# Token tiles of even and of odd tokens as the stationary operand of four projections in a hybrid encoder block

## The chip, the cores and the metric

One NeuronCore of a Trainium2 chip runs the whole block as one program. The metric is the device time of one execution in microseconds (us); the times shown are the median of several executions and their spread. A trace of one profiled execution lists every instruction of the engines: PE (TensorE, the matmuls), PEld (TensorE's weight loads, which overlap PE), DVE (VectorE), ACT (ScalarE), POOL (GpSimd) and SP (SyncE, which issues DMAs).

## The reference

The input is x, 256 tokens of 2048 channels, in fp32. The block computes, cut to what matters here:

```python
proj = x @ w_in                       # q, k, v, r, two small ranks, hyena's u, gate logits
y_gla = gla_branch(q, k, v, r, ...)   # gated linear attention, 4 heads, both directions
y_hy  = hyena_branch(u, ...)          # short convolution, two long convolutions
g = sigmoid(gate_logits)              # (256, 2, 2048)
merged = g[:, 0] * (y_gla @ w_gla_o) + g[:, 1] * (y_hy @ w_hy_o)
h = layernorm(ALPHA * x + merged @ w_out)
out = layernorm(ALPHA * h + square(relu(h @ w_ff1)) @ w_ff2)
```

Four of these products concern the change: the two halves of the gate logits (x with 2048 columns of `w_in` each), `y_gla @ w_gla_o` and `y_hy @ w_hy_o`. Each is 256 tokens x 2048 x 2048. Between them and `merged @ w_out` stand only operations on single elements, so that the order of the tokens is free there.

## The kernel before, in words

**Precision.** Every large product is made in a rounded fp32 (`fp32r`) with split operands: a value is cast to a high part, and the rest is kept as a low part. A product then is three matmuls, high x high, high x low and low x high, that add up in one PSUM tile.

**Activations** lie transposed: `act_tile` is [128, 16, 2, 256], that is, 128 channels on the partitions, 16 tiles of channels, high or low part, and 256 tokens side by side, 4 bytes each. `xT` holds x so, `yT` first holds the GLA branch's output (`yg` in the trace) and then Hyena's (`yh`), and `mT` holds the merged branches.

**Weights** come in blocks of 128x2048 (1 MB) over SP's queue; `fetch` splits each into `whi` and `wlo` with two casts on ACT (line 90) and two subtractions on DVE (line 91). There are three raw tiles and three halves of each part, so that a block is split while an earlier one is multiplied.

**Token products.** `token_group` computes a group of 512 output columns for all 256 tokens: two PSUM tiles, one for each tile of 128 tokens, over 16 channel tiles. In `token_half` the stationary operand is a tile of 128 tokens of the activations, and the moving operand is 512 columns of weights. For each channel tile and each token tile there are three matmuls (lines 201 to 203), and each has a weight load of its own of 128x128. A block of weights is 4 channel tiles, so 24 matmuls; a group is 4 blocks, 96 matmuls. The token tiles are the first and the last 128 tokens, so the 128 columns of a load lie side by side.

The groups are, in order: `r` and `v` for GLA, the first gate (`g1_0` to `g1_3`, lines 701 to 706, which are copied out of PSUM into `q_sb` and `k_sb` and later put through a sigmoid), then four rounds of three groups of Hyena's `u` and one group of the GLA output (`go`, line 832, multiplied into the first gate), the second gate (`g2`, line 869, a sigmoid straight out of PSUM), Hyena's output (`ho`, line 893, multiplied by the second gate and added), and `w_out` (`wo`). The trace drops the numbers, so both gates are named `g` there.

`merged` (line 876), one step after each `ho` group, turns that group's four tiles of 128x128 by transposes on PE and splits them into `mT` (lines 90 and 91 again), which `wo` multiplies.

**Other products.** `channel_products` (lines 140 to 158) has the weights stationary and activations moving: eight matmuls of 512 columns (both parts at once, line 151) and eight of 256 (line 155). The first feed-forward product `f` runs so. The GLA scores `s` (line 642) and all transposes are plain fp32.

**Order.** A scheduler sets the order on each engine when the program is built; small pieces of GLA and Hyena work are put between the blocks of the large products (`later`, `pump`).

Of the kernel before, what the change touches and what calls it, by code (L numbers as in the profile page):

```python
# [16 lines left out]
P = 128  # L17
D = 2048
L = 256
NT = L // P  # L20
KT = D // P
# [26 lines left out]
def block_kernel(  # L48
# [34 lines left out]
    def psum_main(name):  # L83
        return mmp.tile([P, 512], F32, tag="mm", name=name)

    def psum_side(name):
        return sdp.tile([P, 512], F32, tag="sd", name=name)

    def split_hi_lo(hi, lo, src):
        return (nc.scalar.copy(hi, src),  # L90
                nc.vector.tensor_tensor(lo, src, hi.bitcast(F32), op=ALU.subtract))  # L91
# [6 lines left out]
    def fetch():  # L98
        n = fetched[0]
        if n >= stop_at[0]:  # L100
            return
        fetched[0] = n + 1
        raw = wp.tile([P, D], F32, tag="raw", bufs=3, name=f"raw{n}")
        nc.sync.dma_start(raw, wblk[n])
        parts = []
        for h in range(2):
            hi, lo = weight_half(n, h)
            last_low[0] = split_hi_lo(hi, lo, raw[:, h * 1024:(h + 1) * 1024])[1]
            parts.append((hi, lo))
        queue.append(parts)  # L110

    def weight_half(n, h):
        return (wp.tile([P, D // 2], F32R, tag="whi", bufs=3, name=f"whi{n}_{h}"),
                wp.tile([P, D // 2], F32R, tag="wlo", bufs=3, name=f"wlo{n}_{h}"))
# [4 lines left out]
    def later(d, fn):  # L119
        clock[1] += 1  # L120
        side.append((clock[0] + d, clock[1], fn))

    def pump():
        clock[0] += 1
        due = sorted((e for e in side if e[0] <= clock[0]), key=lambda e: e[:2])
        for e in due:
            side.remove(e)
        for e in due:
            e[2]()
# [6 lines left out]
    def next_block():  # L136
        fetch()
        return queue.popleft()
# [50 lines left out]
        for h in range(n, 2):  # L189
            channel_products(ps, act, parts[h], range(8 * h, 8 * h + 8))  # L190

    def token_half(pss, act, half, tbs, kt0, ends=(0, KT - 1), order=lambda ins: ins):
        hi, lo = half
        for j in range(2):
            kt = kt0 + j
            wh = hi[:, j * 512:(j + 1) * 512]
            wl = lo[:, j * 512:(j + 1) * 512]
            for tb in tbs:
                sh = act[:, kt, 0, tb * P:(tb + 1) * P]
                sl = act[:, kt, 1, tb * P:(tb + 1) * P]  # L200
                order(MM(pss[tb], sh, wh, start=(kt == ends[0]), stop=False))  # L201
                order(MM(pss[tb], sh, wl, start=False, stop=False))  # L202
                order(MM(pss[tb], sl, wh, start=False, stop=(kt == ends[1])))  # L203

    def token_products(pss, act, blocks, tbs, b0):
        for b, parts in enumerate(blocks):
            for h in range(2):
                token_half(pss, act, parts[h], tbs, (b0 + b) * 4 + h * 2)

    def token_group(act, name):  # L210
        pss = [psum_main(f"{name}_{tb}") for tb in range(NT)]
        for b in range(4):
            token_products(pss, act, [next_block()], range(NT), b)
            pump()
        return pss

# [18 lines left out]
    def act_tile(pool, tag, name):  # L235
        return pool.tile([P, KT, 2, L], F32R, tag=tag, name=name)
# [11 lines left out]
    xT = act_tile(base, "xT", "xT")  # L248
# [7 lines left out]
    with tc.tile_pool(name="xp", bufs=1) as xp, tc.tile_pool(name="xq", bufs=1) as xq:  # L256
# [25 lines left out]
        for i in range(3):  # L282
            t = weight_half(-1, i)
# [224 lines left out]
    for g in range(4):  # L508
        ng = fp.tile([P, 512], F32, tag="ng", name=f"ng{g}")
        nc.scalar.dma_start(ng, norm_g[0:1, g * 512:(g + 1) * 512].broadcast_to([P, 512]))  # L510
        pss = token_group(xT, f"r{g}")
        for tb in range(NT):
            sr = fp.tile([P, 512], F32, tag="sr", name=f"sr{g}{tb}")
            nc.scalar.activation(sr, pss[tb], AF.Silu)
            nc.vector.tensor_tensor(g_sb[:, tb, g * 512:(g + 1) * 512], sr, ng, op=ALU.mult)
# [9 lines left out]
    yT = act_tile(base, "yT", "yg")  # L525
# [159 lines left out]
    for h in range(HEADS):  # L685
        v2 = yT[:, 4 * h:4 * h + 4].rearrange("p k i l -> p (k i l)").rearrange("p (i t d) -> p i t d", i=2, t=NT)
        vh, vl = v2[:, 0], v2[:, 1]
        pss = token_group(xT, f"v{h}")
# [8 lines left out]
    def m_group(g):  # L697
        t = m_sb[g // 2][:, 4 * (g % 2):4 * (g % 2) + 4, :]
        return t.rearrange("p a l -> p (a l)").rearrange("p (t d) -> p t d", t=NT)

    for g in range(4):
        pss = token_group(xT, f"g1_{g}")
        mg = m_group(g)
        with tc.high_priority():
            nc.scalar.copy(mg[:, 0], pss[0])
            nc.vector.tensor_copy(mg[:, 1], pss[1])
# [125 lines left out]
    def gla_o_group():  # L832
        g = go_done[0]
        go_done[0] += 1
        pss = token_group(yT, f"go{g}")
        mg = m_group(g)
        for tb in range(NT):
            nc.vector.tensor_tensor(mg[:, tb], mg[:, tb], pss[tb], op=ALU.mult)

    load_taps(0)  # L840
    for s in range(NCH // 2):
        for k, n in enumerate(("v", "x1", "x2")):
            pss = token_group(xT, f"u{n}{s}")
# [14 lines left out]
    yhT = act_tile(base, "yT", "yh")  # L858
# [10 lines left out]
        later(1 + 2 * c, reload(c))  # L869
    g2_sb = qp.tile([P, 4, NT, 512], F32, tag="G", name="g2_sb")  # L870
    for g in range(4):
        pss = token_group(xT, f"g2_{g}")
        for tb in range(NT):
            nc.scalar.activation(g2_sb[:, g, tb], pss[tb], AF.Sigmoid)
    drain()
    mT = act_tile(base, "xT", "mT")

    def merged(g):
        def run():
            mg = m_group(g)  # L880
            for k2 in range(2):
                pt = psum_side(f"mt{g}{k2}")
                for kk in range(2):
                    for tb in range(NT):
                        kt = 2 * k2 + kk
                        nc.tensor.transpose(
                            pt[:, kk * L + tb * P:kk * L + (tb + 1) * P],
                            mg[:, tb, kt * P:(kt + 1) * P], ident)
                s = slice(4 * g + 2 * k2, 4 * g + 2 * k2 + 2)
                split_hi_lo(mT[:, s, 0], mT[:, s, 1], pt.rearrange("p (a b) -> p a b", a=2))  # L890
        return run

    for g in range(4):
        pss = token_group(yhT, f"ho{g}")
        mg = m_group(g)
        for tb in range(NT):
            gt = g2_sb[:, g, tb]
            nc.vector.tensor_tensor(gt, gt, pss[tb], op=ALU.mult)
            nc.vector.tensor_tensor(mg[:, tb], mg[:, tb], gt, op=ALU.add)
        later(1, merged(g))  # L900
# [18 lines left out]
    def resident_pieces(parts, order=lambda ins: ins):  # L919
        for part in parts:  # L920
            n = fetched[0]
            fetched[0] = n + 1
            raw = wp.tile([P, D], F32, tag="raw", bufs=3, name=f"raw{n}")
            nc.sync.dma_start(raw, wblk[n])
            for h, (hi, lo) in enumerate(part):
                order(split_hi_lo(hi, lo, raw[:, h * 1024:(h + 1) * 1024])[1])
        return parts

    def resident(slots):
        return resident_pieces([[(hi[:, c:c + 1024], lo[:, c:c + 1024]) for c in (0, 1024)] for hi, lo in slots])  # L930

    def halves(pool, tag, name):
        t = pool.tile([P, 4, D], F32R, tag=tag, name=name)
        return [(t[:, 0], t[:, 1]), (t[:, 2], t[:, 3])]
# [62 lines left out]
    for g in range(3):  # L997
        pss = token_group(mT, f"wo{g}")
# [3 lines left out]
    parts = resident([x0] + halves(ep, "f", "wr1"))  # L1002
    pss = [[psum_main(f"wo3_{tb}{ch}") for ch in range(2)] for tb in range(NT)]
# [383 lines left out]
    for g in range(2):  # L1387
        pss = [psum_main(f"w2_3{g}_{tb}") for tb in range(NT)]
        for i, kt in enumerate(at_kt):
            token_half(pss, f3, next_half(), range(NT), kt, ENDS)  # L1390
            if g == 0 and i == 1:
                ff_close(*open_sums)
                rows2 = load_rows(2)
        if g == 0:
            for tb in range(NT):
                add_ff(pss[tb], tb, 0, 512)
# [9 lines left out]
    def quarters(*tiles):  # L1406
        at = [t[:, k:k + 1024] for t in tiles for k in range(0, t.shape[1], 1024)]
        return [[(at[0], at[1]), (at[2], at[3])], [(at[4], at[5]), (at[6], at[7])]]
# [4 lines left out]
    with tc.issue_after(last_low[0].ins):  # L1413
        parts = resident_pieces(quarters(*own, *spare), keep)
# [7 lines left out]
    parts = [half for block in parts for half in block]  # L1422
# [7 lines left out]
    for half, kt in third:  # L1430
        token_half(left, f3, half, [0], kt, ENDS, keep)
# [4 lines left out]
    pss = [psum_main(f"w2_33_1{ch}") for ch in range(2)]  # L1436
# [24 lines left out]
    for at, n in CENTRED[:3]:  # L1461
        po[at] = psum_side(f"lo{at}")
        parts = [(unit, z[:, at:at + 512]) for z in zg] if at < 1024 else [(ident, z1[:, 1, at:at + 512])]
# [4 lines left out]
    with tc.high_priority(), tc.issue_after(done.ins):  # L1468
# [3 lines left out]
        y, t, v, rs = (ep.tile([P, 1], F32, tag=f"fin{i}", name=f"fin{i}") for i in range(4))  # L1472
# [162 lines left out]
```

## Time and profile before

| | us |
|---|---|
| median of 3 runs | 1788.35 |
| lowest and highest | 1787.66, 1789.82 |
| span of the profiled execution | 1785.8 |
| PE busy | 1778.0 |
| DVE busy | 1482.7 |
| ACT busy | 1052.2 |

The profiled execution's own total isn't listed apart; its span, from the first instruction of the program to the last, is 1785.8 us, 2.55 below the median of the runs.

How to read it: the record of a matmul runs from its start to a modelled end and overlaps the next one's, so the pace of PE is read from starts, not from mean durations. In a timeline a row is a start, a length, an engine, a line, an operation, out<-in, the operand's sizes and a count of equal instructions in a row; what stands in brackets is the idle time of the engine before it and what ended that. In a table of groups or of a tile, three numbers with slashes are the shortest, median and longest record in ns. In a table of windows, each engine's busy time stands with its number of instructions. A few matmul records are missing from a trace.

The four products of the change are 16 groups of 96 matmuls, 1536 of the 8739 matmul records.

### The profile page before, as it was taken

How to read it: one execution, taken by the hardware profiler on the slowest of the kernel's cores; microseconds unless marked ns; L12 is line 12 of the kernel's file. 1: busy time of each engine (PE TensorE's matmuls, PEld its weight loads, DVE VectorE, ACT ScalarE, POOL GpSimd, SP SyncE). 2: the span in 40 equal slices, each digit the busy share in tenths (PEclk: the TensorE clock that was granted, in tenths of full speed). 3: DMA queues.
4: the chain of work that ended last, by engine and by line, in shares of the span. 5: the costliest groups of instructions: out<-in, count | busy, mean ns of one | idle time of the engine just before them, and what ended most of it. 6: DMA issues, size and time to landing. Idle time of an engine off the chain costs nothing.

```text
span 1785.8 us, 23513 instructions
## 1 busy us (share of the span) xinstructions
PE 1778.0 (100%) x8739; PEld 1500.6 (84%) x8739; DVE 1482.7 (83%) x1919; ACT 1052.2 (59%) x1418; POOL 180.0 (10%) x234
## 2 busy tenths in 40 slices
PE   9999999999999999999999999999999999999998
PEld 7888888888888888888888889888888888888887
DVE  6789886885679998898755558889999999999998
ACT  6578767875344444444544445676666666666663
POOL 1011110000011201011000000011111111111110
PEclk9999999999999999999999999999999999999999
DMA  8668776445797979798555664687888787888864
GB/s 325 236 241 292 262 233 202 148 165 206 230 288 254 290 232 292 262 289 253 215 184 186 245 263 163 224 247 242 276 248 252 246 264 241 278 240 249 262 217 167
DMA packets 81586, 428.95 MB, mean 240 GB/s; under 512 B 10072, under 2 KB 12648, under 8 KB 40768
## 3 DMA queue, kind: packets, MB, share of 16 engines
q1 hardware_dynamic: 47664, 336.35, 50.5%
q0 software_dynamic: 26608, 71.18, 19.6%
q10 hardware_dynamic: 7200, 19.93, 3.1%
q8 instruction: 68, 1.11, 0.3%
q14 instruction: 46, 0.38, 0.1%
HBM read 383.96 MB, written 16.25 MB: 224 GB/s over the span
## 4 chain that ended last, share of the span: by engine, by line
PE 96%; DVE 3%; DMA 0%; issue 0%; ACT 0%; SPq 0%; DVEq 0%
PE f L151 12%; PE f L155 6%; PE w L1266 5%; PE w L1265 5%; PE w L1264 5%; PE g L202 3%; PE g L201 3%; PE g L203 3%; PE ux L203 3%; PE ux L202 3%; PE ux L201 3%; PE r L201 2%; PE r L203 2%; PE r L202 2%; PE k L151 2%; PE v L202 2%
## 5 line engine op out<-in xcount | busy, mean ns | idle before, releaser
L90 ACT CAST whi<-raw 128x1024 fp32r<-128x1024 f32 x360 | 379.1, 1054 | 382.6 <-PE ux L203 89.3
L91 DVE TENSOR_TENSOR wlo<-raw,whi 128x1024 fp32r<-128x1024 f32 x360 | 438.0, 1220 | 186.5 <-ACT whi L90 183.4
L151 PE MATMUL f<-hT,whi 128*128 128x512 f32 x984 | 243.9, 391 | 0.0
L151 PEld LDWEIGHTS f<-hT,whi 128*128 128x128 f32 x984 | 180.8, 188 | 35.0
L1122 DVE TENSOR_TENSOR wlo<-fraw,whi 128x1024 fp32r<-128x1024 f32 x112 | 136.7, 1221 | 14.3 <-ACT whi L1125 11.0
L155 PEld LDWEIGHTS f<-hT,wlo 128*128 128x128 f32 x984 | 126.2, 191 | 4.8
L155 PE MATMUL f<-hT,wlo 128*128 128x256 f32 x984 | 127.7, 283 | 0.0
L1125 ACT CAST whi<-ring 128x1024 fp32r<-128x1024 f32 x56 | 59.1, 1055 | 113.1 <-DVE ring L1122 113.1
L1185 POOL DMA_DIRECT2D ring<-wblk x56 | 48.6, 868 | 722.6 <-DVE ring L1122 722.6
L1125 ACT CAST whi<-fraw 128x1024 fp32r<-128x1024 f32 x112 | 117.7, 1051 | 0.0
L1125 ACT CAST b_h<-ring 128x1024 fp32r<-128x1024 f32 x112 | 87.9, 834 | 24.0 <-PE w L1266 21.9
L202 PE MATMUL g<-wlo,xT 128*128 128x512 f32 x256 | 100.1, 391 | 0.0
L203 PE MATMUL ux<-whi,xT 128*128 128x512 f32 x256 | 99.9, 390 | 0.0
L203 PE MATMUL g<-whi,xT 128*128 128x512 f32 x256 | 99.9, 390 | 0.0
L202 PE MATMUL ux<-wlo,xT 128*128 128x512 f32 x256 | 99.6, 389 | 0.0
L201 PE MATMUL g<-whi,xT 128*128 128x512 f32 x256 | 93.8, 392 | 0.0
L201 PE MATMUL ux<-whi,xT 128*128 128x512 f32 x256 | 89.7, 389 | 0.0
L1122 DVE TENSOR_TENSOR ring<-ring 128x512 f32<-128x512 f32 x112 | 77.0, 687 | 1.9
L1122 DVE TENSOR_TENSOR b_l<-ring,b_h 128x1024 fp32r<-128x1024 f32 x56 | 68.3, 1219 | 9.1 <-ACT b_h L1125 9.0
L1122 DVE TENSOR_TENSOR wlo<-ring,whi 128x1024 fp32r<-128x1024 f32 x56 | 68.6, 1224 | 2.6 <-ACT whi L1125 0.6
L1122 DVE TENSOR_TENSOR fa<-ring,fa 128x1024 fp32r<-128x1024 f32 x56 | 68.2, 1217 | 0.0
L1186 POOL DMA_DIRECT2D ring<-ring x56 | 67.6, 1207 | 0.0
(515 smaller groups left out, 4299.5 us busy)
## 6 DMA issues: line engine op xcount, KB each, us to landing
raw<-wblk SPq DMA_DIRECT2D x188, 1024.0 KB, 5.3
fraw<-wblk SPq DMA_DIRECT2D x56, 1024.0 KB, 4.8
ring<-wblk SPq DMA_DIRECT2D x56, 1024.0 KB, 6.7
ring<-wblk POOLq DMA_DIRECT2D x56, 256.0 KB, 4.4
ring<-ring POOLq DMA_DIRECT2D x56, 256.0 KB, 5.0
Td<-T POOLq DMA_DIRECT2D x32, 384.0 KB, 5.4
conv_sb<-conv_rows SPq DMA_DIRECT2D x12, 1024.0 KB, 11.5
Tl<-Td POOLq DMA_DIRECT2D x16, 768.0 KB, 9.2
```

Of the source, the lines that this page charges most:

```text
L90: return (nc.scalar.copy(hi, src), nc.vector.tensor_tensor(lo, src, hi.bitcast(F32), op=ALU.subtract))
L91: nc.vector.tensor_tensor(lo, src, hi.bitcast(F32), op=ALU.subtract))
L151: MM(ps[:, :, ts], hi[:, js], act[:, kt, :, ts], start=(kt == 0 and opens), stop=(kt == KT - 1))
L155: MM(ps[:, 0, ts], lo[:, js], act[:, kt, 0, ts], start=False, stop=False)
L201: order(MM(pss[tb], sh, wh, start=(kt == ends[0]), stop=False))
L202: order(MM(pss[tb], sh, wl, start=False, stop=False))
L203: order(MM(pss[tb], sl, wh, start=False, stop=(kt == ends[1])))
L1122: return pin(nc.vector.tensor_tensor(dst, a, b, op=op))
L1125: return pin(nc.scalar.copy(hi, src))
L1264: pin(MM(ps, sh, wh, start=(p == begin), stop=False))
L1265: MM(ps, sh, wl, start=False, stop=False)
L1266: pin(MM(ps, sl, wh, start=False, stop=(p == end - 1)))
```

## The change

The token tiles of those four products are no longer the first and the last 128 tokens, but the even and the odd ones: `act[:, kt, part, tb:256:2]`. The 128 columns of a weight load lie 8 bytes apart in place of 4. The compiled load walks its columns from the last to the first, with a step of -1 before and of -2 now. Gates and branch outputs all have the same order of tokens, so that the products of single elements need no edit. `merged` puts the tokens back in order: it reads its transposed tiles as before and writes them to `mT` at every second place, so `wo` and all after it are as before.

The core of the diff:

```diff
-    def token_half(pss, act, half, tbs, kt0, ends=(0, KT - 1), order=lambda ins: ins):
+    def token_half(pss, act, half, tbs, kt0, ends=(0, KT - 1), order=lambda ins: ins, by_parity=False):
...
             for tb in tbs:
-                sh = act[:, kt, 0, tb * P:(tb + 1) * P]
-                sl = act[:, kt, 1, tb * P:(tb + 1) * P]
+                tokens = slice(tb, L, 2) if by_parity else slice(tb * P, (tb + 1) * P)
+                sh = act[:, kt, 0, tokens]
+                sl = act[:, kt, 1, tokens]
...
-        pss = token_group(xT, f"g1_{g}")
+        pss = token_group(xT, f"g1_{g}", by_parity=True)
...
-        pss = token_group(yT, f"go{g}")
+        pss = token_group(yT, f"go{g}", by_parity=True)
...
-        pss = token_group(xT, f"g2_{g}")
+        pss = token_group(xT, f"g2_{g}", by_parity=True)
...
-                split_hi_lo(mT[:, s, 0], mT[:, s, 1], pt.rearrange("p (a b) -> p a b", a=2))
+                by_token = [mT[:, s, i].rearrange("p a (m t) -> p a t m", t=NT) for i in range(2)]
+                split_hi_lo(*by_token, pt.rearrange("p (a t m) -> p a t m", a=2, t=NT))
...
-        pss = token_group(yhT, f"ho{g}")
+        pss = token_group(yhT, f"ho{g}", by_parity=True)
```

`token_products` and `token_group` pass the new argument on. `r`, `v`, `u`, `wo` and the last feed-forward products keep tiles of tokens that lie side by side. On each engine, the built program has the same instructions in the same order as before.

More of the change, by code (lines that the diff above doesn't have):

```diff
@@ L203, in token_half, with token_products, token_group @@
                 order(MM(pss[tb], sl, wh, start=False, stop=(kt == ends[1])))
-    def token_products(pss, act, blocks, tbs, b0):
+    def token_products(pss, act, blocks, tbs, b0, by_parity=False):
         for b, parts in enumerate(blocks):
             for h in range(2):
-                token_half(pss, act, parts[h], tbs, (b0 + b) * 4 + h * 2)
-    def token_group(act, name):
+                token_half(pss, act, parts[h], tbs, (b0 + b) * 4 + h * 2, by_parity=by_parity)
+    def token_group(act, name, by_parity=False):
         pss = [psum_main(f"{name}_{tb}") for tb in range(NT)]
         for b in range(4):
-            token_products(pss, act, [next_block()], range(NT), b)
+            token_products(pss, act, [next_block()], range(NT), b, by_parity)
             pump()
```

## The prediction

> **What bounds the kernel now.** I read the page first, for which engine ends the span.
>
> ```profile
> PE 1778.0 (100%) x8739; PEld 1500.6 (84%) x8739; DVE 1482.7 (83%) x1919; ACT 1052.2 (59%) x1418; POOL 180.0 (10%) x234
> PEclk9999999999999999999999999999999999999999
> PE 96%; DVE 3%; DMA 0%; issue 0%; ACT 0%; SPq 0%; DVEq 0%
> ```
>
> TensorE (PE) is busy through the whole span at the full granted clock, and the chain that ends last is 96% PE. The waits of PE come next: do its matmuls ever wait for weights to be split?
>
> ```profile
> PE warm L272 <- DVE ones_sb L334: 1.5, 1, 1.5
> PE open L296 <- ACT whi-1_2_133 L308: 0.9, 1, 0.9
> ```
>
> 2.4 us in all, at the opening. So the span is the number of matmuls times the step from one matmul to the next, and the question is what a step holds. The mean ns of a group is no help, because a matmul's record (389 ns here) overlaps the next. I took the starts from the timeline, PE alone. Here are two rows of `ho` (128x512, fp32r), with 44 steps between them:
>
> ```profile
> 1003.95 0.39 PE L202 MATMUL ho<-wlo,yh 128*128 128x512 f32 x1
> ...
> 1013.93 0.39 PE L202 MATMUL ho<-wlo,yh 128*128 128x512 f32 x1
> ```
>
> 9.98 / 44 gives 226.8 ns a step. For a second width I took the chain in order of time, where `channel_products` runs 256-wide matmuls (L155) in rows of 16:
>
> ```profile
> 1127.49 1.91 PE f L155 x16
> 1129.41 3.65 PE f L151 x16
> ```
>
> 1129.41 - 1127.49 over 16 is 120.0 ns. From 256 to 512 columns a step grows by 106.8 ns, or 0.417 ns a column. 256 columns take 106.8 ns of the 120.0, and 13.2 ns are left over; at 512 columns the same 13.2 are left (226.8 - 213.6). So each fp32r matmul here pays 13.2 ns that don't go with its width. Every one has its own weight load, so I looked for matmuls with a weight load of the same 128 columns and another pace. The plain fp32 ones are such:
>
> ```profile
> 952.30 1.03 PE L886 MATMUL mt<-ident,q_sb 128*128 128x128 f32 x8
> L886 PE MATMUL mt<-ident,q_sb x16: 270/272/273, 952.3 to 975.7; 128*128 128x128 f32 x16
> 305.15 0.49 PE L642 MATMUL s<-qx,kk 128*128 128x192 f32 x2
> 305.48 0.55 PE L642 MATMUL s<-qi,kk 128*128 128x64 f32 x4
> L642 PEld LDWEIGHTS s<-qi,ka x64: 132/138/138, 304.3 to 404.5; 128*64 128x64 f32 x64
> L642 PEld LDWEIGHTS s<-qx,kk x32: 186/189/192, 304.7 to 405.2; 128*128 128x128 f32 x32
> ```
>
> Eight transposes take 1.03 us, the last of them 0.27: seven steps in 0.76, or 108.6 ns. Two 192-wide matmuls lie 0.33 us before the next, about 163 ns each. The difference, 54 ns for 64 columns, is 0.84 ns a column: these stream at half the pace of fp32r. 192 columns at 0.834 are 160.1 ns, so some 2.4 ns are left over (1.8 at the transposes, whose 128 columns take 106.8). The load itself isn't shorter: 64 columns of it last 138 ns and 128 columns 189, so it too moves at about 0.8 ns a column, or some 105 ns for its 128 columns. A load of 105 ns therefore hides nearly whole behind a stream of half pace, and leaves 13.2 ns behind a stream of full pace, although that stream of 512 columns is twice as long as the load.
>
> One more place shows that these 13.2 ns aren't a constant of the array. The GLA output matmuls (`o`, also 128x512 fp32r) run in rows of twelve:
>
> ```profile
> 315.33 0.39 PE L337 MATMUL o<-yg,sth 128*128 128x512 f32 x1
> ...
> 318.13 0.63 PE L201 MATMUL v<-whi,xT 128*128 128x512 f32 x2
> ```
>
> 2.80 / 12 is 233.3 ns, 6.5 ns more than in `ho`, with the same form and the clock full; only the tiles differ. The waits have no row for them. I read this as interference: the load and the stream read the same memory, and where they meet, the stream loses time; how often they meet depends on how the two walk.
>
> **The change part by part.** Its main edit reaches these matmuls:
>
> ```profile
> L201 PEld LDWEIGHTS g<-whi,xT x256: 187/188/192, 329.3 to 923.7; 128*128 128x128 f32 x128
> L201 PEld LDWEIGHTS go<-whi,yg x128: 187/188/188, 507.0 to 826.6; 128*128 128x128 f32 x128
> L201 PEld LDWEIGHTS ho<-whi,yh x128: 187/188/188, 924.4 to 1013.5; 128*128 128x128 f32 x128
> ```
>
> 512 of line 201, and as many of 202 and 203: 1536. No instruction is added, removed or moved on any engine. Each of these loads now walks 128 columns that lie 8 bytes apart in place of 4; the moving operands are as before. The price of a load of that form is nowhere in the trace, so it is bounded. Downwards, it can at most take away all that doesn't go with the width: 13.2 x 1536 = 20.3 us. The fp32 rows leave 2.4 ns in place, which makes 10.8 x 1536 = 16.6 us. Upwards, the `o` rows show the same form 6.5 ns dearer for its tiles: 10.0 us; and a left-over that doubles with the bytes walked is another 13.2 ns, 20.3 us.
>
> I take the fp32 rows, for this reason. There load and stream advance alike: 4 bytes in about 0.8 ns each. In the fp32r rows the stream goes twice as fast as the load, so that their places shift against each other all the time and meet again and again. With columns 8 bytes apart, the load advances 8 bytes in 0.8 ns and the stream 4 in 0.417: alike again, as in the fp32 rows. If the two meet once, one of them is late by a turn, and from there on they keep out of each other's way. So the term is -16.6 us, and PE is alone on the path there, so that all of it is on the path.
>
> The Trainium skill ("SBUF — State Buffer", Specifications) says that memory lines have 16 bytes and that two hits in each suffice for full bandwidth; a step of 8 bytes still has two. By it the wider step costs nothing in itself, which leaves the sum above as it is; no run here shows it.
>
> The other edit is in `merged`, which now writes `mT` at every second place, so that its columns stand in token order again for `w_out`. Eight casts and eight subtractions are concerned:
>
> ```profile
> L90 ACT CAST mT<-mt x8: 586/591/595, 953.0 to 1021.5; 128x512 fp32r<-128x512 f32 x8
> L91 DVE TENSOR_TENSOR mT<-mt,mT x8: 679/682/684, 954.3 to 1022.9; 128x512 fp32r<-128x512 f32 x8
> 1020.02 1.06 ACT L90 CAST whi<-raw 128x1024 fp32r<-128x1024 f32 x1 [1.67 <-PE wo L203]
> 1014.38 0.62 PE L201 MATMUL wo<-whi,mT 128*128 128x512 f32 x2
> ```
>
> I take them at nothing more. If the strided writes ran at half speed, each cast would cost 0.59 and each subtraction 0.68 more. What hides that: ScalarE sat idle for 1.67 us before a weight cast in this stretch, and the last part of `mT`, which lands at 1022.9 + 0.7 us, is first read by the fourth block of `wo`, three blocks of 24 steps after 1014.38, at 1030.7. That is 7 us of cover, against 2.5 for the last group's two pairs at double length. Without any cover, the sixteen would cost 8 x (0.59 + 0.68) = 10.2 us.
>
> What is late next, once PE is quicker? A block of weights (24 steps) shrinks from 5.44 to 5.18 us, and its split has to follow. The fullest stretch for VectorE (DVE) is that of the short convolutions, where `go` lies:
>
> ```profile
> core 0: us, PE busy (x) PEld busy (x) DVE busy (x) ACT busy (x) POOL busy (x), PEclk, DMA share, GB/s
> 480.00:680.00 200.00, 200.00 (x887) 165.57 (x887) 174.33 (x176) 89.37 (x96) 25.58 (x34) 1.00 0.88 275
> 900.00:995.00 95.00, 95.00 (x431) 78.81 (x430) 52.96 (x54) 40.62 (x45) 0.00 (x0) 1.00 0.53 187
> ```
>
> DVE is busy for 174 of 200 us there, 53 of 95 in the gates and `ho`. In that stretch `go` makes up 96 of every 384 matmuls of the token groups, so PE gains about 1% and DVE goes from 87 to 88%. It has room, but little. If DVE took back all that `go` gains, that is 384 x 10.8 = 4.1 us.
>
> The sum: the profiled execution's span is 1785.8 us; with -16.6 it is 1769.2. The median of the three runs is 1788.35, 2.55 more, which is what lies outside the span or between one run and another, and the change touches neither. So **1771.8 us** is predicted (1788.35 - 16.6 = 1771.75).
>
> **The rivals.** *A: the left-over stays, nothing moves.* It would then be a fixed price of changing the stationary operand at full pace. For it: it is the same 13.2 ns at 256 and at 512 columns. Against it: the `o` rows, which leave 19.7 at the same pace. The time would be that of before, 1788.35. The Trainium skill ("TensorE: Matmul & The Clock Gate", Step-by-step: what each phase is for) says that the weight load has a read port of its own and takes no bandwidth from the running matmul; by that rule a layout of the stationary operand can't matter, which is this rival. The 13.2 and 19.7 ns beside the 2.4 of fp32 don't agree with it well.
>
> *B: slower.* The left-over is the price of the memory that the load walks, paid by the stream: 512 bytes a partition cost 13.2 ns now, and 1024 will cost 26.4. For it: the left-over goes with the load alone and not with the stream's width, and the fp32 rows, whose stream reads half as often, may simply have gaps that hide it. Against it: the `o` loads walk the same 512 bytes and pay half as much again. That gives 20.3 us more, 1808.7; with the half step that `o` shows, 10.0 us, 1798.3. It decides from the point where the new left-over is above 13.2 + 2.3 ns, since 2.3 x 1536 is 3.6 us, or 0.2%, about the least that a measurement of this kernel can tell from no change.
>
> *C: faster, but less.* The strided load meets the stream less often and not never, or DVE takes `go`'s part back. DVE alone makes it 1788.35 - 12.5 = 1775.9; half of the left-over gone everywhere makes it 6.6 x 1536 = 10.1, so 1778.2.
>
> That the change doesn't do what it says is hardly a rival: the form of the loads is written in the program. What could fail is only that their step matters.
>
> **How the numbers follow.** The forecast gets 0.56: two rows with fp32 and one with other tiles speak for interference, but that equal pace ends it is argued and not shown. C gets 0.12, A 0.13, B 0.19. The forecast's own range goes from 1768.0 (all 13.2 ns gone) to 1775.9. The whole range reaches from there over C to A with the spread of the runs, 1790; it leaves out B, 0.19. Faster by over 0.2% has 0.68 (forecast and C), within 0.2% 0.13, slower 0.19.
>
> **What would show it.** In the profile of the changed kernel, the steps of `g`, `go` and `ho` decide: 44 steps of `ho` in 9.5 us (216 ns) are the forecast, 9.98 is A, 10.3 to 10.6 is B. Steps of `r`, `v`, `ux` and `wo`, which keep their loads, should stay at 226.8; if they change too, the reason is another. If DVE takes gain back, PE's waits show rows on `wlo` of several us between 480 and 900, where there are none now. If the `mT` edit costs, its casts and subtractions are longer than 0.6 and 0.7 us and PE waits for them at `wo`. A span that differs while the steps don't would mean that the steps were the wrong place to look.

## The result, and the profile after

| | before | after |
|---|---|---|
| median of 3 runs, us | 1788.35 | 1797.65 |
| lowest and highest | 1787.66, 1789.82 | 1797.34, 1799.53 |
| span of the profiled execution | 1785.8 | 1796.7 |
| PE busy | 1778.0 | 1788.8 |

The changed kernel is slower: the ratio of its runs to those of before is 1.0055 (95% interval 1.0035 to 1.0075), and the medians differ by 9.3 us, where 16.6 us less were forecast. Below are the lines of the page that answer to those shown of before, and then the waits of PE (from where to where, us in all, times, longest):

```profile
PE 1788.8 (100%) x8739; PEld 1510.2 (84%) x8739; DVE 1484.0 (83%) x1919; ACT 1052.3 (59%) x1418; POOL 180.0 (10%) x234
PEclk9999999999999999999999999999999999999999
PE 95%; DVE 3%; DMA 1%; issue 0%; ACT 0%; DVEq 0%; POOL 0%; ACTq 0%
```

```profile
PE warm L273 <- DVE ones_sb L335: 1.5, 1, 1.5
PE hb L430 <- ACT T L458: 0.5, 1, 0.5
PE w L203 <- DVE wr L91: 0.3, 1, 0.3
```

The same number of matmuls at the same full clock keeps PE busy for 10.8 us more, and PE waits for 2.3 us against 2.4. So no wait on another engine has come in between: the matmuls themselves step more slowly. Which ones, the starts in the timeline show. Two rows of `ho` with 44 steps between them, as in the prediction, then two of `wo` with 42 (lines 201 to 203 are now 202 to 204):

```profile
932.98 0.39 PE L203 MATMUL ho<-wlo,yh 128*128 128x512 f32 x1
...
943.25 0.39 PE L203 MATMUL ho<-wlo,yh 128*128 128x512 f32 x1
...
1031.99 0.39 PE L203 MATMUL wo<-wlo,mT 128*128 128x512 f32 x1
...
1041.51 0.39 PE L203 MATMUL wo<-wlo,mT 128*128 128x512 f32 x1
```

`ho` takes 10.27 us for 44 steps, 233.4 ns a step, where it took 226.8. `wo`, whose loads are as before, takes 9.52 / 42 = 226.7. The 256-wide `f` in the chain is at 120.0 ns as before (1139.62 - 1137.70 over 16):

```profile
1137.70 1.91 PE f L155 x16
1139.62 3.65 PE f L151 x16
```

Taken over all matmuls of a group (starts from the trace, steps with a wait left out), the usual step of `g`, `go` and `ho` went from 226.7 to 233.3 ns; on average `g` grew by 6.0 ns, `go` by 6.4 and `ho` by 6.5, and none of the other large groups by over 0.2. Added up over all their steps, `g` takes 4.5 us more, `go` 2.5 and `ho` 2.5, which is 9.5 us. The medians differ by 9.3 and the profiled spans by 10.9 (the three runs' spans go from 1795.3 to 1796.7); the profiled execution's other 1.4 us lie for the most part in a few single long steps of `r` and `w`, whose usual steps are as before. The loads' own records in `ho` are longer too, 193 ns for 188:

```profile
L202 PEld LDWEIGHTS ho<-whi,yh x128: 193/193/193, 932.3 to 1023.8; 128*128 128x128 f32 x128
L90 ACT CAST mT<-mt x8: 626/632/642, 961.7 to 1031.9; 128x512 fp32r<-128x512 f32 x8
L91 DVE TENSOR_TENSOR mT<-mt,mT x8: 681/684/685, 962.9 to 1033.2; 128x512 fp32r<-128x512 f32 x8
```

The other two rows are the strided writes of `mT`: 632 ns a cast for 591, 684 ns a subtraction for 682. Eight casts make 0.3 us on ScalarE, beside the path.

### The profile page after: what moved, and what is told of

Its sections match the earlier page's. It is cut to its first block, busy times and chain, and to the rows that moved or that the text cites. A ratio compares the mean times of both kernels' runs of the same rounds, so it can differ in the third digit from the quotient of the medians.

```text
span 1796.7 us, 23513 instructions
## 1 busy us (share of the span) xinstructions
PE 1788.8 (100%) x8739; PEld 1510.2 (84%) x8739; DVE 1484.0 (83%) x1919; ACT 1052.3 (59%) x1418; POOL 180.0 (10%) x234
## 4 chain that ended last, share of the span: by engine, by line
PE 95%; DVE 3%; DMA 1%; issue 0%; ACT 0%; DVEq 0%; POOL 0%; ACTq 0%
PE f L151 12%; PE f L155 6%; PE w L1266 5%; PE w L1268 5%; PE w L1267 5%; PE g L203 3%; PE g L202 3%; PE g L204 3%; PE ux L203 3%; PE ux L204 3%; PE ux L202 3%; PE ho L203 2%; PE go L204 2%; PE ho L204 2%; PE go L203 2%; PE go L202 2%
## 5 line engine op out<-in xcount | busy, mean ns | idle before, releaser
L1124 DVE TENSOR_TENSOR wlo<-fraw,whi 128x1024 fp32r<-128x1024 f32 x112 | 136.8, 1222 | 14.2 <-ACT whi L1127 10.9
L155 PEld LDWEIGHTS f<-hT,wlo 128*128 128x128 f32 x984 | 126.2, 191 | 4.8
L155 PE MATMUL f<-hT,wlo 128*128 128x256 f32 x984 | 127.7, 283 | 0.0
```

What stands on the lines that cost most here:

```text
L155: MM(ps[:, 0, ts], lo[:, js], act[:, kt, 0, ts], start=False, stop=False)
L1124: return pin(nc.vector.tensor_tensor(dst, a, b, op=op))
```

## The experiments

"Left-over" is used as in the prediction: a step less 0.417 ns for each column of the stream. Before it is 13.3 ns in `ho` and 13.3 for the 256-wide matmuls of `f` (13.2 in the prediction, which rounds); after, the changed groups leave 20.0. "Distance" is the start of the load's columns less the start of the stream in the memory of a partition, modulo 256 bytes. By the addresses in the built program it is 0 for nearly all large products before; `o` (160 bytes) and `X`, a transform in Hyena's filters (224 bytes), are the exceptions. Where a table gives a mean over a group, the steps come from the starts in the trace, without those that hold a wait. Theory M says that the left-over hangs on how load and stream lie to each other; theory S that it hangs on the memory that the load walks, and nothing else; theory E, the forecast's, that it is least where load and stream advance at the same pace. Runs 5 to 8 are one execution each, read for their steps; the others are the medians of four to twelve.

**1. The loads alone.** `mT` is written as before, so `w_out` multiplies tokens in another order than the last step adds them.

```diff
-                by_token = [mT[:, s, i].rearrange("p a (m t) -> p a t m", t=NT) for i in range(2)]
-                split_hi_lo(*by_token, pt.rearrange("p (a t m) -> p a t m", a=2, t=NT))
+                split_hi_lo(mT[:, s, 0], mT[:, s, 1], pt.rearrange("p (a b) -> p a b", a=2))
```

> The 16 groups keep their token tiles of even and odd tokens, and the split of merged writes mT side by side as before, so that the rows of the merged branches reach w_out in the order even, odd (the order of tokens from w_out on is changed). If the loads alone make the change slower, the time is that of the changed kernel, 1797.6 within 1, and the steps of g, go and ho are 233.3 ns. If the strided writes of mT cost something (8 casts and 8 subtractions, at most 10.2 us), it is nearer to 1788.4.

Measured: 1798.85 us, ratio 1.0055 (1.0039 to 1.0072), span 1796.8. The loads alone cost all of it (`go` and `ho` step 233.3 ns again), and the strided writes nothing that shows.

**2. Only the gates strided.** From the run above, `go` and `ho` get their old token tiles back (two lines of the diff).

> Only the two gates (768 of the 1536 matmuls) take the even and the odd tokens, the branch outputs and the writes of mT are as before; so gates and branches are multiplied with tokens in different order. If each strided load costs its own matmul 6.67 ns and nothing else, half the loads give half the price: 768 x 6.67 = 5.1 us, 1793.6. If the price came from one place (the second half of the program, or a buffer that all four products share), it would be 0 or 10 us.

Measured: 1793.24 us, ratio 1.0027 (1.0016 to 1.0037), 5.0 us above the 1788.22 of before measured beside it. Two rows of `g` and two of `ho`, 42 steps each:

```profile
839.99 0.39 PE L203 MATMUL g<-wlo,xT 128*128 128x512 f32 x1
...
849.79 0.39 PE L203 MATMUL g<-wlo,xT 128*128 128x512 f32 x1
...
1005.32 0.39 PE L203 MATMUL ho<-wlo,yh 128*128 128x512 f32 x1
...
1014.84 0.39 PE L203 MATMUL ho<-wlo,yh 128*128 128x512 f32 x1
```

9.80 / 42 is 233.3 ns and 9.52 / 42 is 226.7. The price is one of each strided load, and half the loads cost half.

**3. Activations 32 bytes lower, loads not strided.** Two unused tiles are resized so that `xT` (with `mT`, which takes its place) and `yT` lie 32 bytes lower, while the weights stay. No instruction changes.

```diff
-    base.tile([P, 64], F32, tag="gap0", name="gap0")
+    base.tile([P, 56], F32, tag="gap0", name="gap0")
...
-    base.tile([P, 64], F32, tag="gap1", name="gap1")
+    base.tile([P, 72], F32, tag="gap1", name="gap1")
```

> The kernel before with xT and yT 32 bytes lower in each partition (two unused pads beside them change by 32 bytes), so that stationary and moving operands no longer start at the same place modulo 64; step of the columns 1 throughout. Theory M (load and stream meet, and how often is a matter of where both lie): the 36 token groups on xT and yT, w_out and the last products on fa go to the step of the o groups, 233.3 ns, some 4000 matmuls at 6.7 ns: 25 to 27 us slower, about 1815. Theory S (the left-over grows with the stretch of memory that a load walks, 512 bytes before and 1024 after): no step changes, 1788.4.

Measured: 1816.94 us, ratio 1.0157 (1.0140 to 1.0174). Two rows of `ho`, 40 steps apart, and two of the 256-wide last part of `wo`, 16 steps apart:

```profile
1020.87 0.40 PE L202 MATMUL ho<-wlo,yh 128*128 128x512 f32 x1
...
1030.20 0.40 PE L202 MATMUL ho<-wlo,yh 128*128 128x512 f32 x1
...
1110.75 0.28 PE L969 MATMUL wo<-wr,mT 128*128 128x256 f32 x1
...
1112.62 0.28 PE L969 MATMUL wo<-xh,mT 128*128 128x256 f32 x1
```

`ho` is at 233.3 ns with loads of step 1: the same price as in the change, now in all the token products (232.9 to 233.8 ns in `r`, `v`, `g`, `ux`, `uv`, `go`, `ho` and `wo`). `f`, whose load and stream didn't move against each other, is a control: its 512-wide steps went only from 228.4 to 229.6 ns on average and its 256-wide ones stayed at 119.6. S as the only cause is refuted, since the memory walked is as before. The 256-wide steps of `wo` went the other way, to 116.9 ns from 120.0. So at this distance (224 bytes) the left-over goes with the width of the stream, 20 ns at 512 columns and 10 at 256; at distance 0 it is 13.3 at both.

**4. The changed kernel, 32 bytes lower.** The same two lines in the changed kernel.

> The changed kernel with the same shift of 32 bytes. Theory S: the strided loads keep 233.3 ns and the others 226.7, so 1797.6. Theory M: the token groups with a step of 1 go to 233.3, the strided ones to some other value between 216 and 240 ns that depends on the shift; if they stayed at 233.3 with and without the shift, that would speak for the step of the columns itself in their case, with about 1814.

Measured: 1817.11 us, ratio 1.0158 (1.0143 to 1.0173). The strided groups leave 20 ns here and without the shift (`ho` 233.4 ns on average), where M had first expected another value, and the others now cost what they cost in run 3. A load of step 2 doesn't mind these 32 bytes. And in the shifted layout the change costs nothing: 1817.11 us with it and 1816.94 without.

**5. Everything 32 bytes higher.** One unused tile ahead of all others: stationary and moving operands move together.

```diff
+    base.tile([P, 8], F32, tag="gap3", name="gap3")
     eps_sb = base.tile([P, 1], F32, tag="eps", name="eps_sb")
```

> The program before with an unused tile of 32 bytes ahead of everything: stationary and moving operands of all large products move by 32 bytes together, and start at 64 modulo 256 in place of 32. If only the distance of the two starts matters, every step stays (226.7 ns, span 1785.8 to 1787). If the place of the stationary operand itself matters, the 512-wide steps go to 233.3, as where the activations alone were moved by 32 bytes, and the span to about 1815 or more.

Measured: 1787.14 us. Its page begins:

```profile
span 1785.0 us, 23513 instructions
```

That is the span of before within 0.8 us, and `ho` steps 226.8 ns as before. For this shift only the distance counts, not the place.

**6. The row that the forecast rested on.** The GLA output matmuls `o` are moved from distance 160 to 0, with one unused tile ahead of GLA's.

```diff
+    gp.tile([P, 24], F32, tag="gap2", name="gap2")
     scan_sb = gp.tile([P, 260], F32, tag="scan", name="scan_sb")
```

> The program before with one unused tile of 96 bytes ahead of GLA's tiles, so that the stationary operand of the GLA output matmuls (o) starts with its moving operand modulo 256 bytes, from which it was 160 bytes off. Theory M: twelve steps of o in 2.72 us in place of 2.80 (226.7 ns a step for 233.3), 48 x 6.67 = 0.3 us in all, too little for the total. If o is dear for another reason (its place between other work, its PSUM banks), 2.80 stays.

Measured: 1787.82 us. The first of the twelve and the first matmul behind them:

```profile
315.15 0.39 PE L337 MATMUL o<-yg,sth 128*128 128x512 f32 x1
...
317.87 0.61 PE L201 MATMUL v<-whi,xT 128*128 128x512 f32 x2
```

2.72 us for twelve, 226.7 ns, where before took 2.80. Over all 48 the mean left-over fell from 19.8 to 13.5 ns, and no instruction changed but for its addresses. So `o` was dear because of its distance.

**7. A scan of steps and starts.** The 24 groups of `u`, `go`, `g2` and `ho` each load with a step and a start of their own, so that they multiply other columns; the stream is as before.

> One look at 24 groups, each with its own step of the stationary columns and its own start (off), the same matmuls otherwise; the stationary columns are other numbers of the same tile, so v, x1, x2, the gates and the branch outputs are computed from other columns. Theory S: the left-over depends on the step alone and grows with it: 13.3 ns at 1, 20 at 2, more at 3 to 16. Theory M: it depends on the start as well (off 8 floats at a step of 1 gives 20 ns, off 16 gives 13.3 again), and it is not monotone in the step: some steps give less than 13.3.

Measured: 1804.97 us. Rows of three groups, 40 steps apart: step 1 at start 0, step 2, step 8.

```profile
443.78 0.39 PE L214 MATMUL uv<-wlo,xT 128*128 128x512 f32 x1
...
452.85 0.39 PE L214 MATMUL uv<-wlo,xT 128*128 128x512 f32 x1
...
465.61 0.39 PE L214 MATMUL ux<-wlo,xT 128*128 128x512 f32 x1
...
474.94 0.39 PE L214 MATMUL ux<-wlo,xT 128*128 128x512 f32 x1
...
671.29 0.41 PE L214 MATMUL ux<-wlo,xT 128*128 128x512 f32 x1
...
681.07 0.41 PE L214 MATMUL ux<-wlo,xT 128*128 128x512 f32 x1
```

These are 226.8, 233.3 and 244.5 ns a step. The mean left-over of the groups, with those that run 8 added at 512 columns (start in columns of 4 bytes):

| load step | start: left-over, ns |
|---|---|
| 1 | 0: 13.3; 1: 19.1; 2: 17.4; 4: 15.0; 8: 19.8; 12: 19.8; 16: 20.0; 24: 20.7; 32: 19.0; 48: 15.5; 56: 19.9; 60: 13.4; 63: 13.3; 64: 14.0; 72: 20.0; 128: 13.9 |
| 2 | 0: 20.0; 1: 20.0; 4: 20.0; 8: 19.3; 12: 17.9; 32: 18.0 |
| 3; 4 | 22.1 and 26.5; 21.7 and 24.4 |
| 5; 6; 7; 8; 16 | 23.6; 24.2; 25.3; 31.6; 22.3 |

Of what was tried, only step 1 reaches the low of 13.3 ns, at distance 0 or 4 and 16 bytes short of it, and nearly again (14.0 and 13.9) 256 and 512 bytes on. The wider the step, the more is left by and large, but not evenly, and far less than in proportion to the memory walked (step 2 leaves 20.0, not 26.6). S fails here again.

**8. Width and pace.** The same with 256- and 128-wide matmuls, with a stream of step 2, and with strided loads in the fp32 transposes.

> The program before, with the 24 groups of u, go, g2 and ho each given its own form (so that they multiply other columns): the load's step and start, the stream's width (256- and 128-wide matmuls in place of 512, in twice or four times the number) and the stream's step. And the transposes of the merged branches (plain fp32) with a load of step 1, 2, 4 and 3 in the four groups. Theory M (a stream pays 3 columns in 32 unless load and stream start alike modulo 256 bytes): 256-wide matmuls leave 32 cycles at start 0 and 24 at all other starts and at step 2, 128-wide ones no more than that; 512-wide ones leave 48 at starts 32, 48, 56, 60 and 63 columns on, and 32 at 128. With a stream of step 2, no load matches and all leave 48 or more. Theory E (the forecast's: equal pace ends the interference) has the lowest left-over where both walk 8 bytes a column, load step 2 and stream step 2, and more at load step 1 and 4. Theory S (the price goes with the memory that the load walks): 48 at step 2 at any width. The fp32 transposes step 108.6 ns with step 1; S expects more with 2, 3 and 4, M and E about the same at 2, because a stream of half pace leaves room for the load.

Measured: 1999.31 us, for the many narrow and half-pace matmuls. Rows in this order: 256-wide with load step 1 at start 0 and at start 2 (80 steps each), 256-wide with load step 4 (24), 128-wide with load step 1 (80) and 2 (32), and 512-wide with a stream of step 2 (40).

```profile
442.18 0.40 PE L217 MATMUL uv<-whi,xT 128*128 128x256 f32 x2
...
451.78 0.40 PE L217 MATMUL uv<-wlo,xT 128*128 128x256 f32 x2
...
464.73 0.39 PE L217 MATMUL ux<-wlo,xT 128*128 128x256 f32 x2
...
473.97 0.62 PE L217 MATMUL ux<-whi,xT 128*128 128x256 f32 x4
...
717.99 0.63 PE L217 MATMUL ux<-wlo,xT 128*128 128x256 f32 x2
...
723.59 0.63 PE L217 MATMUL ux<-wlo,xT 128*128 128x256 f32 x2
...
848.25 0.61 PE L217 MATMUL uv<-wlo,xT 128*128 128x128 f32 x4
...
857.19 0.61 PE L217 MATMUL uv<-wlo,xT 128*128 128x128 f32 x4
...
941.04 1.10 PE L217 MATMUL ux<-whi,xT 128*128 128x128 f32 x8
...
944.81 0.63 PE L217 MATMUL ux<-wlo,xT 128*128 128x128 f32 x4
...
521.67 1.07 PE L217 MATMUL go<-whi,yg 128*128 128x512 f32 x2
...
539.78 0.64 PE L217 MATMUL go<-wlo,yg 128*128 128x512 f32 x1
```

256-wide steps take 120.0 ns at distance 0 and 115.5 at 8 bytes, less away from distance 0 as M expected; with load step 4 they take 233.3 ns, which is as long as a 512-wide step, and the load's own record is 329 ns there, where step 1 at start 0 has 192. 128-wide ones take 111.8 ns at step 1 and 117.8 at step 2. At 128 columns, and at step 4, the step no longer follows the stream; what binds there I take to be the load. A stream of step 2 runs at half pace: 18.11 / 40 is 452.8 ns. In that half-pace stream the mean steps are 453 and 452 ns with load step 1 (two starts), 453 with load step 2 and 459 with load step 4. Then the fp32 transposes, eight with load step 1 and eight with step 2:

```profile
1161.18 1.03 PE L917 MATMUL mt<-ident,q_sb 128*128 128x128 f32 x8
1184.18 1.11 PE L917 MATMUL mt<-ident,q_sb 128*128 128x128 f32 x8
```

From the first start to the eighth, seven steps take 0.76 us and 0.83 (the last record is 0.27 and 0.28 long): 109 ns and 118; loads of step 3 and 4 give 117 and 119. Theory E, the forecast's, fails twice: step 2 on both sides is no low, and a strided load costs time beside an fp32 stream too. M, which had expected no change there, is wrong on this point. M had also expected any load to leave 10 ns at 256 columns; with step 2 the group leaves 13.4, and the other starts at step 1 leave 8.9 to 13.0. At 512 columns three of its starts came out lower than it said (48, 60 and 63, in the table above).

**9. Step 2 where the stream is 256 wide.** In the program before, the low weights of the later `f` rows are written in pairs of blocks and loaded with step 2.

```diff
+                if low_apart:
+                    first = kt % 8 // 2 * 2 * P + kt % 2
+                    js = slice(first, first + 2 * P - 1, 2)
                 MM(ps[:, 0, ts], lo[:, js], act[:, kt, 0, ts], start=False, stop=False)
...
-        rest(lo, src, hi)
+        in_pairs = [t.rearrange("p (k t j) -> p k t j", t=2, j=P) for t in (src, hi)]
+        rest(lo.rearrange("p (k j t) -> p k t j", t=2, j=P), *in_pairs)
```

> The program before, with one edit elsewhere: in the 56 later rows of the first feed-forward product the low weights (the stationary operand of the 256-wide matmuls of line 155) are written in pairs of blocks, column by column in turn, and loaded with step 2. 56 x 16 = 896 matmuls. If the price of a load that isn't in step with the stream goes with the stream's width (48 cycles at 512 columns, 24 at 256, as in the program moved by 32 bytes), a 256-wide matmul gets cheaper by step 2, from 32 cycles to 24: 896 x 3.33 ns = 3.0 us, 1785.5. If step 2 adds 16 cycles to any matmul, because the load walks twice the memory, it gets 896 x 6.67 = 6.0 us dearer, 1794.5. Strided writes of the low weights on VectorE are expected at nothing by both.

Measured: 1788.28 us, ratio 0.9999 (0.9990 to 1.0007), and 16 of these matmuls still take 1.91 us:

```profile
1127.77 1.91 PE f L158 x16
```

Neither expectation held. At 256 columns a load of step 2 costs as much as one of step 1 at distance 0, which the scan above shows too. Step 2 costs at 512 columns and not at 256, so its price is no fixed sum for a load.

**10. The gain that run 3 pointed to.** In the program before, with all tokens side by side, the low weights of `f` (the load of the 256-wide matmuls) start 8 bytes later. To have the room, each such tile is 64 columns longer, the two unused tiles are gone, and GLA's mask lies in GLA's pool.

```diff
-                wp.tile([P, D // 2], F32R, tag="wlo", bufs=3, name=f"wlo{n}_{h}"))
+        lo = wp.tile([P, D // 2 + 64], F32R, tag="wlo", bufs=3, name=f"wlo{n}_{h}")
+        at = LOW_START if n in LOW_SHIFTED else 0
+        return hi, lo[:, at:at + D // 2]
```

> The program before, with all token tiles as they were. The halves of the low weights get 64 columns more (256 bytes), and where they are the stationary operand of 256-wide matmuls (line 155 in the first feed-forward product, 1008 matmuls) they start 2 columns (8 bytes) later, so that load and stream no longer start alike modulo 256 bytes. For room, two unused tiles of 256 bytes are gone and a mask of GLA lies in GLA's own pool. Theory M: 256-wide matmuls that started 2 columns on left 21.4 cycles in the second scan in place of 32, so 1008 x 10.6 cycles at 2.4 GHz is 4.5 us off, 1783.8. Rival: in rows of eight between rows of eight 512-wide matmuls the time is given back, or the low weights, written 8 bytes off, take longer on VectorE: 1788.2 or more.

> The same layout with the larger halves and the moved mask, but the low weights start where they did: the layout alone. Both theories: as before, 1788.2 within 0.1%. What it differs from that is not to be put down to the start of the loads in the run beside it.

Measured: 1785.22 us, ratio 0.9984 (0.9975 to 0.9993), faster than both kernels. Its interval has no 1 in it. The layout alone: 1787.56 us, ratio 0.9995 (0.9985 to 1.0004). The chain of the first, in order of time (L155 is the 512-wide high product there, L159 the 256-wide low one):

```profile
1133.65 3.68 PE f L155 x16
1137.33 1.86 PE f L159 x16
1139.19 3.68 PE f L155 x16
```

Sixteen low products take 1.86 us for 1.91, and sixteen high ones 3.68 for 3.65. Over all of them, and against the kernel before, the mean 256-wide left-over of `f` fell from 12.9 to 9.8 ns (3.5 us in 1104), the 512-wide one of `f` rose by 1.0 ns (1.0 us in 984) and that of `w` by 0.2 (0.2 us in 1344). The rest, 2.3 us, is what lies between the medians of the two runs. What the layout alone does to these steps isn't shown. The start of the load does give time, and the expected 4.5 us was too much: a 256-wide matmul gains less here than in the scan, and its neighbours pay some of it back, as the rival had it in part.

## Why the prediction was wrong

**What held.** PE alone set the end, and the span followed the count of matmuls times their step: some 9.5 us of steps, where the medians differ by 9.3. The groups that kept their loads kept their steps. The `mT` edit cost nothing, with 41 ns a cast hidden; DVE took nothing back and had nothing to take. The `o` rows were rightly read as a matter of where load and stream lie: run 6 moved the loads by 96 bytes and the steps fell to 226.7 ns. The bound that these rows gave, 6.5 ns and 10.0 us, was the size of what came: rival B with "the half step that `o` shows", 1798.3, is within 1 us of the median. That is luck as far as its reason goes: `o` paid for its distance and the change for its step, and no run shows why both come to 20 ns.

**The step that failed** is the one that gave the term its sign: with columns 8 bytes apart "the load advances 8 bytes in 0.8 ns and the stream 4 in 0.417: alike again, as in the fp32 rows", and from there the two keep out of each other's way. Equal pace brings no low. At 512 columns a load of step 2 leaves 20.0 ns in the changed kernel and 17.9 to 20.0 at the starts tried (runs 4, 7 and 8), where the forecast put 2.4, and a stream of step 2 beside it is no better (run 8). The fp32 rows were no evidence for it: their 2.4 ns lie beside a stream of half pace, and there, too, a strided load costs some 9 ns. The comparison of speeds also left out the direction. The compiled load goes from its last column to its first, and the compiled stream goes upwards, so that the two run towards each other: at equal pace they don't keep their distance, in either kernel. No run turned a walk round, so what this does to the time isn't shown.

**What was overlooked** is that 13.3 ns is itself the low. The kernel before lies so that load and stream start alike modulo 256 bytes in nearly every large product; run 3 lost 28 us by 32 bytes. The prediction set the `o` rows against `ho` and left it at "only the tiles differ". The addresses of those tiles would have said that `o` is 160 bytes off and `ho` none, and so that `ho` might already lie at the best place. The trace of before holds a second such pair: `X`, 224 bytes off, steps 233.5 ns at 512 columns and 117.2 at 256, as run 3 has it for `wo`. So the left-over of `X` does go with the width, and 13.2 ns is no price that every fp32r matmul pays. Rival B's own reason, that the left-over doubles with the memory walked, is wrong too, by size (20.0 for 26.4) and by runs 3 and 6. A slip of the working on which nothing hangs: 51 ns for 64 columns make about 102 ns for a load of 128, not 105.

Both rules of the Trainium skill that the prediction weighed fail to give these times. By the Trainium skill ("SBUF — State Buffer", Specifications) two hits in a 16-byte line suffice for full bandwidth; the same row also says that each cross to a new line pays a penalty, which the prediction left out. Here a load with two columns in 16 bytes costs 6.67 ns beside a 512-wide stream, and a stream with two columns in 16 bytes takes 452.8 ns for 226.7. By the Trainium skill ("TensorE: Matmul & The Clock Gate", Step-by-step: what each phase is for) the load has its own read port and takes no read bandwidth from the running matmul. Here 32 bytes of distance cost 28 us all the same.

**What stays open.** Why distance 0 is a low for step 1 and step 2 has none wasn't settled. That load and stream meet in parts of the memory that repeat every 256 bytes would fit the period, but it is argued and not shown. Nor is it shown why the left-over goes with the stream's width away from distance 0 and not at it, or why matmuls with a load of step 4 step 233 ns in fp32r and 119 in fp32.

## What to carry to other kernels

When PE alone sets the end, read the step from starts and ask what of it doesn't go with the width; if two groups of the same form differ, compare the addresses of their operands modulo a few hundred bytes before you reason about the engine. A row that is dearer than its neighbour bounds the loss, but it takes a row that is cheaper to make a gain likely: here no 512-wide fp32r group left less than 13 ns, and that should have weighed more than the mechanism. An unused tile of 32 bytes is an experiment that changes no instruction, and it settles such a question in one run.

## What the runs showed of the hardware

- In the token products, an fp32r matmul of 512 columns with a load of step 1 steps about 227 ns if the load's columns start where the stream starts, modulo 256 bytes (or 4 or 16 bytes short of it), and 228 to 234 at the other starts tried. One of 256 columns is the other way round: 120.0 ns at that place, 115.5 to 119.7 at the others, with the least at 8 bytes.
- A stationary operand of step 2 costs up to 6.67 ns at 512 columns and nothing at 256, each against step 1 at distance 0. With step 4 a 256-wide matmul steps 233.3 ns, and the load's record is 329 ns for 192; that the matmul waits for the load there is argued from these two.
- A moving operand of step 2 halves the pace of fp32r: 452.8 ns for 512 columns.
- 128-wide fp32r matmuls with a load each step some 111.8 ns at both starts tried, and 117.8 with a load of step 2.
